# Down product of a decoder step: block results added in pairs by VectorE, other places for plain jobs, buffers shared with the gated layer

## The chip, the cores and the metric

The kernel runs on one core of one Trainium2 chip. The metric is the device time of one execution in microseconds (us), the median of several runs. The engines are TensorE (PE: matmuls; PEld: its weight loads), VectorE (DVE), ScalarE (ACT), GpSimd (POOL) and SyncE (SP), which issues most DMA transfers.

## What is computed

One step of a decoder layer over 512 prompt tokens and 8 x 8 sample tokens, T = 576 columns in all, in float32. Cut to what matters here:

```
u = rms_norm(x, g_mix) @ w_in                 # 2048 -> three mixers' inputs
y_a = short_conv(u_a); y_b = ssd(u_b, dt_bias, a_log, ...); y_c = sparse_attention(u_c)
x = x + concat(rms_norm(y_a), rms_norm(y_b), rms_norm(y_c)) @ w_out
h = rms_norm(x, g_ffn)
x = x + (silu(h @ w_gate) * (h @ w_up)) @ w_down      # 2048 -> 5632 -> 2048
```

## The kernel before

All products run on TensorE with the weights as the stationary operand and 288 of the 576 columns (HALF) as the moving one. A float32 operand is held as two parts, `hi` (made by ScalarE, a copy to fp32r) and `lo` (made by VectorE, operand minus `hi`); one product is hi\*hi + hi\*lo + lo\*hi, so three matmuls for each 128 rows. `split` (line 130) makes the pair.

**Input projection.** `run_jobs` (line 441) runs jobs of 96 matmuls, one for 128 columns of `w_in`, in three lists: `jobs1`, `jobs2`, `jobs3`. Between the matmuls of a job `pump.run(369.0 * len(job.halves) * ratio)` lets `Pump` (line 38) take steps of side work worth that many estimated nanoseconds. The side work is `chain` (line 1664): compress, `sample_attn` (eight batches), `prompt_attn`, `merge_c`. A ratio of 0.85 (`jobs2`) or 1.05 (`jobs3`) sets how much side work goes in for each main matmul, and so how dense the main matmuls lie in the instruction order. Each engine then executes its own list in order.

**Out projection.** `jobs4` multiplies the merged mixers (S4, S3) by `w_out`, with `ssd` (line 1189) and `merge_a` as side work. `ssd` begins with 16 short VectorE operations on `sd`, which need the loads `dtb` (dt_bias) and `ea` (exp of a_log), issued there on SyncE's queue (lines 1194, 1196).

**Gated layer.** `w_gate` and `w_up` are multiplied block-wise by a 2 x 2 scheme of seven products instead of eight. An item is seven products of 12 matmuls, 84 in all; there are 88 items. `prep` makes each product's weight pair; the pairs lie in pool `wpool` (tags whi, wlo, 3 buffers) for three of seven products and in pool `fw` (fhi, flo, 4 buffers) for the others, chosen by a running count (line 1905). Raw weights come in `fw`'s `wr` (5 buffers). The result g goes to DRAM (`g_d`). The pool `fw` is closed at line 1986, before the down product's tiles are opened.

**Down product.** 5632 rows of `w_down` are cut into 16 plain jobs on the first 4 row tiles (`jobs6[0]`, 24 matmuls each), three ranges of twelve tiles, of which eight tiles go through the seven-product scheme (eight items of 84 matmuls, product order "1256473") and four tiles are again 16 plain jobs, and 16 last plain jobs, behind which the output rows are transposed and stored (`out_rows`). In one item:

- `w_ops` makes the seven weight pairs: four VectorE additions of weight blocks (`ws`, `wr`) and seven `lo` subtractions (tile f), from raw tiles `wr` (8 buffers of 128 columns).
- `evac_d` (line 2094) takes each product's sum out of PSUM: x1T (the running result, in SBUF) gets products 2, 3, 4 and 5 by VectorE directly; product 1 goes by ScalarE into u, u becomes 1+6 and then 1+6+7 by VectorE, and GpSimd adds u to x1T three times in an item (two of 288 columns, one of 576).
- PSUM: products 1, 2, 5 in `pt` (3 buffers), 6 and 4 in the two halves of one `pg` tile, 7 in `po`, 3 in a second `pg` tile.

Plain jobs stand behind items of odd number (`mp % 2`, four of eight) in the first two ranges; the other twelve of a range run behind it, mixed with `range_ops` of the next range, which builds that range's 28 combinations of g (tile go). `g_in` loads and splits the four tiles of g for the next plain jobs (tile ghl).

Of the kernel before, what the change touches and what calls it, by code (L numbers as in the profile page):

```python
# [76 lines left out]
def hybrid_step_kernel(ctx, tc, x_prompt, x_sample, cache_k, cache_v, cache_win_k, cache_win_v,  # L77
# [238 lines left out]

    rstdB = consts.tile([128, T], F32, name="rstdB")

    ssq = consts.tile([128, 5], F32, name="ssq")
# [121 lines left out]
    def run_jobs(jobs, ratio):  # L441
        for job in jobs:
            run_group([job], ratio)
# [745 lines left out]
    def ssd():  # L1189
        YB = dp.tile([128, 4, T], F32, name="YB")  # L1190
        sq_b = sq_c
        tiny = lambda name, n=8: dp.tile([128, 5, n], F32, name=name)
        dtb = dp.tile([128, 8], F32, name="dtb")
        nc.sync.dma_start(dtb, dram(dt_bias, 0, [[0, 128], [1, 8]]))
        ea = dp.tile([128, 8], F32, name="ea")
        nc.sync.dma_start(ea, dram(a_log, 0, [[0, 128], [1, 8]]))
        dsk = dp.tile([128, 4], F32, name="dsk")
# [489 lines left out]
    run_jobs(jobs1[2:], 0.8)  # L1687
    run_jobs(jobs2, 0.85)
    run_jobs(jobs3, 1.05)
    pump.drain(main)  # L1690
# [189 lines left out]
    def prep(i):  # L1880
# [16 lines left out]
        for n in "1264375":  # L1897
            if g < NE and n in "12":
                continue
            if n == "6":  # L1900
                s2 = ws(s1, a11, OP.subtract)
            if n == "3":
                s4 = ws(a12, s2, OP.subtract)
            src = {"1": a11, "2": a12, "6": s2, "4": a22, "3": s4, "7": s3, "5": s1}[n]
            p = n_op[0] % 7
            n_op[0] += 1
            pool, pre, bufs = (wpool, "w", 3) if p < 3 else (fw, "f", 4)
            hi = pool.tile([128, KC, 128], F32R, name=pre + "hi", tag=pre + "hi", bufs=bufs)
            lo = pool.tile([128, KC, 128], F32R, name=pre + "lo", tag=pre + "lo", bufs=bufs)
            split(hi, lo, src)  # L1910
            out.append((n, hi, lo))
            tick(600)
            yield
# [71 lines left out]

    close_pool(fwg)
    x1g, x1p = open_pool("x1")
# [14 lines left out]
    def out_rows(m):  # L2002
# [3 lines left out]
        ot = evt(512).rearrange("p (a b) -> p a b", a=4)  # L2006
        ots = fp.tile([128, 128], F32, name="ots", tag="ots", bufs=2)
        ps = pt()
# [54 lines left out]
    def load_d(i):  # L2063
        if i >= len(items):
            return
        r, mp = items[i]
        loaded[i] = []
        for h in range(2):
            for q_ in range(2):
                w = fp.tile([128, KC, 128], F32, name="wr", tag="wr", bufs=8)  # L2070
                nc.sync.dma_start(w, dram(w_down, (12 * r + 4 + 4 * h) * 128 * D + mp * 256 + q_ * 128,
                                          [[D, 128], [128 * D, KC], [1, 128]]))
                loaded[i].append(w)

    def w_ops():

        for i in range(len(items)):
            a11, a21, a12, a22 = loaded.pop(i)
            s1 = fp.tile([128, KC, 128], F32, name="ws", tag="ws", bufs=2)
            for n in ORDER:  # L2080
# [6 lines left out]
                src = {"1": a11, "2": a12, "3": a12, "4": a22, "5": s1, "6": a11, "7": a21}[n]  # L2087
                hi, lo = [fp.tile([128, KC, 128], F32R, name=f"f{q_}", tag=f"f{q_}", bufs=4) for q_ in range(2)]
                split(hi, lo, src)
# [3 lines left out]

    def evac_d(mp, n, p, u):

        m = mp * 2
        x11, x21, x12 = x1T[:, m, :HALF], x1T[:, m + 1, :HALF], x1T[:, m, HALF:]
        if n == "1":
            act(u, p)
            tt(x11, x11, u, OP.add, G)  # L2100
        elif n == "2":
            tt(x11, p, x11, OP.add)
        elif n == "5":
            x2 = x1T[:, m:m + 2, HALF:]
            tt(x2, p[:, None, :].to_broadcast([128, 2, HALF]), x2, OP.add)
        elif n == "6":
            tt(u, p, u, OP.add)
            tt(x12, x12, u, OP.add, G)
        elif n == "4":
            tt(x21, p, x21, OP.add)  # L2110
        elif n == "7":
            tt(u, p, u, OP.add)
            x2 = x1T[:, m + 1].rearrange("p (h t) -> p h t", h=2)
            tt(x2, x2, u[:, None, :].to_broadcast([128, 2, HALF]), OP.add, G)
        else:
            tt(x12, p, x12, OP.add)

# [30 lines left out]
    for r in range(NR):  # L2148
        rest = list(jobs6[1 + r])
        tiles = list(range(plain[1 + r], plain[1 + r] + 4))  # L2150
        for mp in range(KT // 2):
            if r + 1 == NR and mp == 7:
                tiles = list(range(plain[-1], nf))
            i = r * KT // 2 + mp
            u = evt(HALF)
            pa, pb = pg(), pg()
            ps = [pt()[:, :HALF] for _ in range(3)] + [pa[:, 0, :HALF], pa[:, 1, :HALF], po()[:, :HALF], pb[:, 0, :HALF]]
            for p, n in zip(ps, ORDER):
                next(weights, None)
                hi, lo = made.pop((i, n))  # L2160
                for j in range(KC):
                    o = ops[r, j, n]
                    for c_, (w, x) in enumerate(((hi, o[:, 0]), (hi, o[:, 1]), (lo, o[:, 0]))):
                        PE.matmul(p, w[:, j, :], x, start=(j == 0 and c_ == 0), stop=(j == 3 and c_ == 2))  # L2164
                evac_d(mp, n, p, u)
                if tiles and (n in "53" or r + 1 == NR):
                    g_in(tiles.pop(0))

            for _ in range((2, 2, 2, 2, 3, 3, 2, 0)[mp] if r + 1 == NR else mp % 2):
                run_group([rest.pop(0)], 0.0)  # L2170
# [10 lines left out]
    close_pool(fg)  # L2181
    close_pool(x1g)
    close_pool(eg)

# [28 lines left out]
```

## Time and profile before

| | us |
|---|---|
| median of 3 runs (2987.16 to 2991.98) | 2990.16 |
| the profiled execution | 2989.67 |
| its span, first to last instruction | 2987.9 |
| TensorE busy | 2837.6 (95%) |
| VectorE busy | 2170.7 (73%) |
| ScalarE busy | 1283.3 (43%) |
| GpSimd busy | 641.2 (21%) |

By the time line the input projection lasts from 0 to about 1150 us (sample attention 500 to 800, prompt attention to 1130), the out projection from 1150 to 1340, the gated layer from about 1520 to 2426, the down product from 2426 to the end. A window's row gives, for each engine, busy us and in brackets the instructions that began in it. At full clock TensorE does 77 matmuls in 10 us, so a row with fewer tells what was lost, by waiting or by a lower clock.

### The profile page before, as it was taken

To read this page: it belongs to the slowest core of one execution; us is meant where nothing else is said; L and a number is where in the kernel's file an instruction comes from. 1 tells how busy PE (TensorE), PEld (TensorE's weight loads), DVE (VectorE), ACT (ScalarE), POOL (GpSimd) and SP (SyncE) were. 2 spreads that over 40 slices of the span, in tenths; PEclk is the share of its full clock that TensorE was granted. 3 is DMA by queue.
4 is the path that set the end of the run, shared out by engine and by line. 5 is a ranking of instruction groups with operands and counts; after the bars stand their busy time and mean duration, and the time that the engine had idled before them with its cause. 6 is when DMAs were issued, how large, how long until landed. Compare 5 with 4: busy or idle time off the path is not lost.

```text
span 2987.9 us, 57523 instructions
## 1 busy us (share of the span) xinstructions
PE 2837.6 (95%) x22006; PEld 2729.2 (91%) x22006; DVE 2170.7 (73%) x4409; ACT 1283.3 (43%) x2432; POOL 641.2 (21%) x672
## 2 busy tenths in 40 slices
PE   7999998787899998999999999999999999999999
PEld 6999997676789887999999999999999999999998
DVE  5566565444586765757899988888888879889874
ACT  5465563222354553335554444444444434444332
POOL 2342342444343320202001101101101102222120
PEclk9999999898999998999999999999999999999999
DMA  7444333554623214357655433333333354333323
GB/s 234 117 130 124 94 90 84 166 161 144 151 60 79 58 50 138 105 159 215 185 182 172 161 101 108 109 106 108 107 109 109 108 180 125 118 103 118 110 70 111
DMA packets 485660, 370.65 MB, mean 124 GB/s; under 512 B 70121, under 2 KB 444880, under 8 KB 485384
## 3 DMA queue, kind: packets, MB, share of 16 engines
q1 hardware_dynamic: 461656, 306.55, 35.2%
q0 software_dynamic: 20944, 55.13, 6.4%
q10 hardware_dynamic: 2784, 5.29, 0.5%
q8 instruction: 174, 2.85, 0.4%
q14 instruction: 102, 0.84, 0.1%
HBM read 312.98 MB, written 51.79 MB: 122 GB/s over the span
## 4 chain that ended last, share of the span: by engine, by line
PE 49%; DVE 5%; DMA 2%; issue 1%; ACT 1%; SPq 0%; POOL 0%; ACTq 0%; DVEq 0%
PE pg L1949 16%; PE pg L434 12%; PE pt L1949 9%; PE po L1949 5%; PE pg L2164 2%; PE pt L2164 2%; DVE f L96 1%; PE pt L434 1%; PE po L2164 1%; DVE wlo L96 1%; DVE x1T L96 1%; DMA raw<-in_w_up_dram 1%; DMA u<-g_d 1%; DVE wr L96 0%; PE pt L128 0%
## 5 line engine op out<-in xcount | busy, mean ns | idle before, releaser
L93 ACT ACTIVATE whi<-raw 128x512 fp32r<-128x512 f32 (+1 forms) x510 | 319.4, 628 | 536.8 <-PE pg L434 260.7
L96 DVE TENSOR_TENSOR wlo<-raw,whi 128x512 fp32r<-128x512 f32 (+1 forms) x510 | 354.1, 696 | 171.3 <-ACT whi L93 143.3
L434 PE MATMUL pg<-hhi,whi 128*128 128x288 f32 (+1 forms) x1440 | 344.6, 319 | 4.8 <-issue 4.0
L1949 PE MATMUL pg<-X,fhi 128*128 128x288 f32 x1656 | 333.6, 297 | 0.5 <-DVE u L96 0.5
L434 PE MATMUL pg<-hlo,whi 128*128 128x288 f32 (+1 forms) x1440 | 326.0, 306 | 8.1 <-issue 4.7
L434 PE MATMUL pg<-hhi,wlo 128*128 128x288 f32 (+1 forms) x1440 | 324.1, 305 | 7.3 <-issue 4.3
L1949 PEld LDWEIGHTS pg<-X,fhi 128*128 128x128 f32 x1656 | 264.8, 188 | 4.5 <-DVE u L96 0.7
L96 POOL TENSOR_TENSOR u<-u 128x576 f32<-128x576 f32 x44 | 70.9, 1616 | 888.3 <-DVE u L96 811.2
L434 PEld LDWEIGHTS pg<-hhi,whi 128*128 128x128 f32 (+1 forms) x1440 | 238.0, 196 | 20.7 <-issue 17.0
L434 PEld LDWEIGHTS pg<-hlo,whi 128*128 128x128 f32 (+1 forms) x1440 | 241.8, 196 | 13.5 <-issue 8.7
L434 PEld LDWEIGHTS pg<-hhi,wlo 128*128 128x128 f32 (+1 forms) x1440 | 241.5, 196 | 9.6 <-issue 5.9
L93 ACT ACTIVATE fhi<-raw 128x512 fp32r<-128x512 f32 x246 | 155.3, 632 | 212.1 <-PE pg L1949 180.9
L1949 PE MATMUL pg<-X,flo 128*128 128x288 f32 x828 | 239.3, 295 | 0.0
L1949 PE MATMUL pt<-X,whi 128*128 128x288 f32 x1168 | 235.8, 295 | 0.0
L434 PE MATMUL pg<-ghl,whi 128*128 128x288 f32 x1280 | 228.8, 298 | 3.9 <-DVE ghl L96 2.6
L96 DVE TENSOR_TENSOR flo<-raw,fhi 128x512 fp32r<-128x512 f32 x246 | 170.2, 693 | 46.3 <-ACT fhi L93 41.9
L434 PE MATMUL pg<-S,whi 128*128 128x288 f32 x1024 | 197.1, 301 | 0.4 <-DVE u L96 0.4
L434 PEld LDWEIGHTS pg<-ghl,whi 128*128 128x128 f32 x1280 | 190.1, 190 | 4.9 <-DVE ghl L96 2.8
L1949 PEld LDWEIGHTS pt<-X,whi 128*128 128x128 f32 x1168 | 188.2, 188 | 0.0
L96 POOL TENSOR_TENSOR x1T<-x1T,u 128x288 f32<-128x288 f32 (+1 forms) x72 | 99.1, 1376 | 392.7 <-ACT u L93 240.5
L1949 PE MATMUL pt<-X,wlo 128*128 128x288 f32 x584 | 172.9, 296 | 0.0
L434 PEld LDWEIGHTS pg<-S,whi 128*128 128x128 f32 x1024 | 159.0, 191 | 1.4 <-issue 0.6
(1343 smaller groups left out, 6979.0 us busy)
## 6 DMA issues: line engine op xcount, KB each, us to landing
wr<-in_w_gate_dram SPq DMA_DIRECT2D x88, 512.0 KB
wr<-in_w_up_dram SPq DMA_DIRECT2D x88, 512.0 KB
raw<-in_w_in_dram SPq DMA_DIRECT2D x144, 256.0 KB
wr<-in_w_down_dram SPq DMA_DIRECT2D x96, 256.0 KB
raw<-in_w_down_dram SPq DMA_DIRECT2D x80, 256.0 KB
raw<-in_w_out_dram SPq DMA_DIRECT2D x64, 256.0 KB
g_d<-u POOLq DMA_DIRECT2D x44, 288.0 KB
u<-g_d SPq DMA_DIRECT2D x40, 288.0 KB
```

What stands on the lines that cost most here:

```text
L93: S.activation(out, in_, func, bias=bias, scale=scale, accum_out=accum)
L96: (eng or V).tensor_tensor(out, a, b, op=op)
L434: PE.matmul(ps[:m, s, :HALF], w[:, k, :m], x[:, s * HALF:(s + 1) * HALF], start=(k0 + k == 0 and n == 0), stop=(k0 + k == n_k - 1 and n == 2))
L1949: PE.matmul(P[n], w[:, k, :], xx, start=(j == 0 and q_ == 0), stop=(j == 7 and q_ == 2))
L2164: PE.matmul(p, w[:, j, :], x, start=(j == 0 and c_ == 0), stop=(j == 3 and c_ == 2))
```

## The change

1. `ea` and `dtb` become constants of the program, loaded on GpSimd's queue near its start, and not inside `ssd` on SyncE's queue.
2. The ratios of `jobs2` and `jobs3` go from 0.85 to 0.95 and from 1.05 to 1.1: more side work for each main matmul, so the chain ends earlier in the order and more main matmuls are left behind it.
3. The gated layer's last item takes its first three products from `wpool` and its last four from `fw`.
4. `fw` stays open. The down product's raw weights lie in its `wr` (5 buffers of 256 columns), and its weight pairs in its fhi, flo (4 buffers).
5. `ots`, the staging tile of the sample rows, has one buffer and not two.
6. `evac_d` uses no GpSimd. Products 2 and 3 share one `pg` tile and are added to x1T by one VectorE addition of 576 columns; product 1 and 1+6 lie side by side in u and are added in one addition of 576; 1+6+7 is made in a tile v and added in one of 576. Product 4 is in `po`, 1, 5, 6 and 7 are in `pt`.
7. Plain jobs stand behind six of eight items (`mp % 4 > 0`) in the first two ranges, and in the last range as (0, 2, 3, 4, 4, 3, 0, 0) and not (2, 2, 2, 2, 3, 3, 2, 0). Ten jobs, not twelve, then carry `range_ops`, three steps each. The tiles of g for the last jobs are asked for from item 6 on, and always behind products 5 and 3.

```diff
+    nc.gpsimd.dma_start(ea, dram(a_log, 0, [[0, 128], [1, 8]]))
+    nc.gpsimd.dma_start(dtb, dram(dt_bias, 0, [[0, 128], [1, 8]]))
...
-        nc.sync.dma_start(dtb, dram(dt_bias, 0, [[0, 128], [1, 8]]))
-        nc.sync.dma_start(ea, dram(a_log, 0, [[0, 128], [1, 8]]))
...
-    run_jobs(jobs2, 0.85)
-    run_jobs(jobs3, 1.05)
+    run_jobs(jobs2, 0.95)
+    run_jobs(jobs3, 1.1)
...
-            p = n_op[0] % 7
+            p = n_op[0] % 7 if i + 1 < len(items) else len(out)
...
-    close_pool(fwg)
...
-        ots = fp.tile([128, 128], F32, name="ots", tag="ots", bufs=2)
+        ots = fp.tile([128, 128], F32, name="ots", tag="ots", bufs=1)
...
+            w2 = fw.tile([128, KC, 256], F32, name="wr", tag="wr", bufs=5).rearrange("p a b -> p (a b)")
...
-                w = fp.tile([128, KC, 128], F32, name="wr", tag="wr", bufs=8)
+                w = w2[:, q_ * KC * 128:(q_ + 1) * KC * 128].rearrange("p (k c) -> p k c", k=KC)
...
-                hi, lo = [fp.tile([128, KC, 128], F32R, name=f"f{q_}", tag=f"f{q_}", bufs=4) for q_ in range(2)]
+                hi, lo = [fw.tile([128, KC, 128], F32R, name=q_, tag=q_, bufs=4) for q_ in ("fhi", "flo")]
...
         if n == "1":
-            act(u, p)
-            tt(x11, x11, u, OP.add, G)
-        elif n == "2":
-            tt(x11, p, x11, OP.add)
+            act(u[:, :HALF], p)
...
-            tt(u, p, u, OP.add)
-            tt(x12, x12, u, OP.add, G)
+            tt(u[:, HALF:], p, u[:, :HALF], OP.add)
...
-            tt(u, p, u, OP.add)
+            v = evt(HALF)
+            tt(v, p, u[:, HALF:], OP.add)
             x2 = x1T[:, m + 1].rearrange("p (h t) -> p h t", h=2)
-            tt(x2, x2, u[:, None, :].to_broadcast([128, 2, HALF]), OP.add, G)
-        else:
-            tt(x12, p, x12, OP.add)
+            tt(x2, x2, v[:, None, :].to_broadcast([128, 2, HALF]), OP.add)
+            tt(x1T[:, m], x1T[:, m], u, OP.add)
+        elif n == "3":
+            tt(x1_, p23, x1_, OP.add)
...
-            pa, pb = pg(), pg()
-            ps = [pt()[:, :HALF] for _ in range(3)] + [pa[:, 0, :HALF], pa[:, 1, :HALF], po()[:, :HALF], pb[:, 0, :HALF]]
+            pa = pg()
+            p1, p5, p6 = [pt()[:, :HALF] for _ in range(3)]
+            ps = [p1, pa[:, 0, :HALF], p5, p6, po()[:, :HALF], None, pa[:, 1, :HALF]]
...
-            for _ in range((2, 2, 2, 2, 3, 3, 2, 0)[mp] if r + 1 == NR else mp % 2):
+            for _ in range((0, 2, 3, 4, 4, 3, 0, 0)[mp] if r + 1 == NR else mp % 4 > 0):
```

Two places show how the order moves. The first is TensorE in one down item, from the end of product 6 to the start of product 3. Before (f_29520 and f_29521 are product 6's pair, f_29559 and f_29560 product 7's, f_29537 and f_29538 product 4's):

```order
L2164 MATMUL pg<-go,f_29521 128x288
L2164 MATMUL po<-go,f_29559 128x288 [waits Activation_49]
...
L2164 MATMUL po<-go,f_29559 128x288 x2
L2164 MATMUL pg<-go,f_29537 128x288 [waits DVE_49]
...
L2164 MATMUL pg<-go,f_29538 128x288
L2164 MATMUL po<-go,f_29560 128x288
...
L2164 MATMUL pg<-go,f_29577 128x288 [waits Activation_49]
```

Now, products 4 (po), 7 (pt) and 3 (pg) of an item:

```order
L2165 MATMUL po<-go,fhi 128x288 [waits Activation_49]
L2165 MATMUL po<-go,fhi 128x288
L2165 MATMUL po<-go,flo 128x288 [waits DVE_49]
...
L2165 MATMUL pt<-go,fhi 128x288 [waits Activation_49]
L2165 MATMUL pt<-go,fhi 128x288
L2165 MATMUL pt<-go,flo 128x288 [waits DVE_49]
...
L2165 MATMUL pg<-go,fhi 128x288 [waits Activation_49]
L2165 MATMUL pg<-go,fhi 128x288
L2165 MATMUL pg<-go,flo 128x288 [waits DVE_49]
```

Before, product 4's first matmul waits for VectorE, which must first have taken product 6 out of the same tile, and product 7's twelve matmuls are cut in two around it; now each product waits for nothing but its own weights.

The second is VectorE where the out projection begins: the last evacuations of the input projection (x<-pg) and the head of `ssd`'s operations on sd. Before:

```order
L96 TENSOR_TENSOR wlo<-raw,whi 128x512 [waits DMAHW6_49,DMAHW7_49,PE_49,Activation_49]
L96 TENSOR_TENSOR x_13438<-pg,x_13438 128x288 [waits DMAHW0_49,PE_49]
L96 TENSOR_TENSOR x_13446<-pg,x_13446 128x288 [waits DMAHW2_49,DMAHW1_49]
L96 TENSOR_TENSOR x_13439<-pg,x_13439 128x288 [waits DMAHW3_49,PE_49]
L96 TENSOR_TENSOR sd_13534<-dtg,dtb 128x40 [waits DMAHW3_49]
L96 TENSOR_TENSOR x_13447<-pg,x_13447 128x288 [waits DMAHW5_49,DMAHW4_49]
L105 SCALAR_TENSOR_TENSOR sd_13535<-sd_13534 128x40 [waits DVE_49]
```

Now:

```order
L96 TENSOR_TENSOR wlo<-raw,whi 128x512 [waits DMAHW6_49,Activation_49]
L96 TENSOR_TENSOR u<-u,rstdB 128x576 [waits DVE_49]
L1412 COPY u<-cols_198 128x8x2
L96 TENSOR_TENSOR sd_13534<-dtg,dtb 128x40
L100 TENSOR_SCALAR triU<-diff 128x128
L105 SCALAR_TENSOR_TENSOR sd_13535<-sd_13534 128x40 [waits DVE_49]
L100 TENSOR_SCALAR sd_13539<-sd_13534 128x40
```

The sd operations no longer wait for a load, and they stand ahead of the input projection's last evacuation and not behind the out projection's first results (the x<-pg). On TensorE, 201 main matmuls of the input projection now stand behind the last matmul of `merge_c`, where 54 stood; and in each of the eight batches of the sample attention 96 main matmuls stand where 108 stood.

## Rows read from the trace of the kernel before

**Rows 1.** Windows by stage: sample attention, then prompt attention and its end.
```profile
500.00:780.00 280.00, 216.55 (x2044) 178.61 (x2040) 116.13 (x327) 61.93 (x114) 123.81 (x130) 0.85 0.51 153
860.00:1150.00 290.00, 285.12 (x2384) 257.92 (x2383) 204.69 (x649) 143.79 (x361) 88.93 (x89) 1.00 0.26 61
```

**Rows 2.** Windows (PE, PEld, DVE, ACT, POOL; PEclk): start of the out projection.
```profile
1150.00:1195.00 45.00, 32.40 (x179) 30.04 (x178) 25.47 (x80) 9.22 (x20) 5.22 (x6) 0.73 0.69 200
...
1165.00:1170.00 5.00, 5.00 (x40) 5.00 (x39) 0.82 (x2) 0.21 (x1) 0.00 (x0) 1.00 0.66 193
```

**Rows 3.** Waits in 1145 to 1200: engine, line, what ended it: us, times, longest.
```profile
ACT ea L93 <- DMA ea<-in_a_log_dram: 6.9, 1, 6.9
...
PE pt L120 <- DVE sd L105: 6.6, 1, 6.6
...
PE pg L434 <- DVE wlo L96: 4.9, 1, 4.9
```

**Rows 4.** Time line of VectorE there: start, duration, operation.
```profile
1172.35 0.19 DVE L96 TENSOR_TENSOR sd<-dtg,dtb 128x40 f32<-128x40 f32 x1
...
1178.30 0.20 DVE L105 SCALAR_TENSOR_TENSOR sd<-sd,ea 128x40 f32<-128x40 f32 x1
```

**Rows 5.** Time line of SyncE's queue there: the next weights of the out projection.
```profile
1176.51 1.92 SPq L1721 DMA_DIRECT2D raw<-in_w_out_dram  x3
```

**Rows 6.** Waits of TensorE, 500 to 820.
```profile
PE po L120 <- issue: 14.8, 27, 1.8
```

**Rows 7.** Windows over the down product.
```profile
2426.00:2590.00 164.00, 155.68 (x1121) 153.04 (x1120) 143.26 (x235) 67.58 (x125) 35.07 (x27) 0.97 0.52 158
2590.00:2750.00 160.00, 156.81 (x1165) 154.97 (x1165) 144.56 (x241) 66.04 (x125) 35.33 (x25) 1.00 0.37 109
2750.00:2910.00 160.00, 160.00 (x1197) 159.11 (x1196) 127.10 (x204) 58.32 (x105) 29.24 (x21) 1.00 0.32 94
```

**Rows 8.** Windows of 10 us at four places of it.
```profile
2420.00:2430.00 10.00, 6.96 (x50) 6.37 (x48) 5.21 (x8) 2.92 (x5) 3.20 (x3) 0.97 0.73 234
2430.00:2440.00 10.00, 9.31 (x51) 9.31 (x52) 4.70 (x8) 1.60 (x4) 1.08 (x3) 0.69 0.87 287
...
2580.00:2590.00 10.00, 8.23 (x51) 8.00 (x50) 7.70 (x15) 3.54 (x7) 1.36 (x2) 0.83 0.69 223
...
2910.00:2920.00 10.00, 8.78 (x66) 8.55 (x65) 6.77 (x11) 4.93 (x8) 2.01 (x2) 1.00 0.45 146
...
2940.00:2950.00 10.00, 10.00 (x79) 9.89 (x78) 4.95 (x9) 3.43 (x6) 0.00 (x0) 1.00 0.46 133
```

**Rows 9.** Waits in 2400 to 2988.
```profile
PE pg L2164 <- DVE u L96: 8.4, 9, 1.8
...
ACT go L93 <- DMA u<-g_d: 6.9, 4, 2.2
```

**Rows 10.** Time line of ScalarE and of VectorE where the down product begins.
```profile
2426.07 0.63 ACT L93 ACTIVATE whi<-raw 128x512 fp32r<-128x512 f32 x1 [7.48 <-PE po L1949]
...
2428.69 3.95 DVE L96 TENSOR_TENSOR ghl<-go,ghl 128x576 fp32r<-128x576 f32 x4
```

**Rows 11.** VectorE's groups by form, 2490 to 2580 (seven items).
```profile
L96 DVE TENSOR_TENSOR f<-wr,f 128x512 fp32r<-128x512 f32 x40 | 28.3, 710 | 0.3
L96 DVE TENSOR_TENSOR f<-ws,f 128x512 fp32r<-128x512 f32 x7 | 13.5, 1923 | 0.0
...
L96 DVE TENSOR_TENSOR wr<-ws,wr 128x512 f32<-128x512 f32 x7 | 7.3, 1039 | 0.2
...
L96 DVE TENSOR_TENSOR x1T<-pt,x1T 128x576 f32<-128x576 f32 x7 | 5.2, 750 | 0.4 <-PE pt L2164 0.2
```

**Rows 12.** Time line of VectorE in an item, 2510.
```profile
2510.14 1.92 DVE L96 TENSOR_TENSOR f<-ws,f 128x512 fp32r<-128x512 f32 x1
2511.98 0.44 DVE L96 TENSOR_TENSOR x1T<-pg,x1T 128x288 f32<-128x288 f32 x1
```

**Rows 13.** Time line of GpSimd there.
```profile
2509.70 1.81 POOL L96 TENSOR_TENSOR x1T<-x1T,u 128x576 f32<-128x576 f32 x1 [3.07 <-DVE u L96]
```

More of the change, by code (lines that the diff above doesn't have):

```diff
@@ L317, in hybrid_step_kernel @@
     rstdB = consts.tile([128, T], F32, name="rstdB")
+    ea = consts.tile([128, 8], F32, name="ea")
+    dtb = consts.tile([128, 8], F32, name="dtb")
+    nc.gpsimd.dma_start(ea, dram(a_log, 0, [[0, 128], [1, 8]]))
+    nc.gpsimd.dma_start(dtb, dram(dt_bias, 0, [[0, 128], [1, 8]]))
     ssq = consts.tile([128, 5], F32, name="ssq")
@@ L1192, in ssd @@
         tiny = lambda name, n=8: dp.tile([128, 5, n], F32, name=name)
-        dtb = dp.tile([128, 8], F32, name="dtb")
-        nc.sync.dma_start(dtb, dram(dt_bias, 0, [[0, 128], [1, 8]]))
-        ea = dp.tile([128, 8], F32, name="ea")
-        nc.sync.dma_start(ea, dram(a_log, 0, [[0, 128], [1, 8]]))
         dsk = dp.tile([128, 4], F32, name="dsk")
@@ L2092, in w_ops, with evac_d @@
             load_d(i + 2)
-    def evac_d(mp, n, p, u):
+    def evac_d(mp, n, p, u, p23):
         m = mp * 2
-        x11, x21, x12 = x1T[:, m, :HALF], x1T[:, m + 1, :HALF], x1T[:, m, HALF:]
+        x21, x1_ = x1T[:, m + 1, :HALF], x1T[:, m].rearrange("p (h t) -> p h t", h=2)
         if n == "1":
-            act(u, p)
-            tt(x11, x11, u, OP.add, G)
-        elif n == "2":
-            tt(x11, p, x11, OP.add)
+            act(u[:, :HALF], p)
         elif n == "5":
@@ L2151, in hybrid_step_kernel @@
         for mp in range(KT // 2):
-            if r + 1 == NR and mp == 7:
+            if r + 1 == NR and mp == 6:
                 tiles = list(range(plain[-1], nf))
             i = r * KT // 2 + mp
-            u = evt(HALF)
-            pa, pb = pg(), pg()
-            ps = [pt()[:, :HALF] for _ in range(3)] + [pa[:, 0, :HALF], pa[:, 1, :HALF], po()[:, :HALF], pb[:, 0, :HALF]]
+            u = evt(T)
+            pa = pg()
+            p1, p5, p6 = [pt()[:, :HALF] for _ in range(3)]
+            ps = [p1, pa[:, 0, :HALF], p5, p6, po()[:, :HALF], None, pa[:, 1, :HALF]]
             for p, n in zip(ps, ORDER):
+                p = pt()[:, :HALF] if p is None else p
                 next(weights, None)
@@ L2164, in hybrid_step_kernel @@
                         PE.matmul(p, w[:, j, :], x, start=(j == 0 and c_ == 0), stop=(j == 3 and c_ == 2))
-                evac_d(mp, n, p, u)
-                if tiles and (n in "53" or r + 1 == NR):
+                evac_d(mp, n, p, u, pa[:, :, :HALF])
+                if tiles and n in "53":
                     g_in(tiles.pop(0))
-            for _ in range((2, 2, 2, 2, 3, 3, 2, 0)[mp] if r + 1 == NR else mp % 2):
+            for _ in range((0, 2, 3, 4, 4, 3, 0, 0)[mp] if r + 1 == NR else mp % 4 > 0):
                 run_group([rest.pop(0)], 0.0)
@@ L2182, in hybrid_step_kernel @@
     close_pool(x1g)
+    close_pool(fwg)
     close_pool(eg)
```

## The prediction

> **What bounds the kernel now.** I read the stages first. In the gated layer, which the change leaves alone but for its last item, TensorE has no gap; the time can only move where it has. The windows over the down product [rows 7] give the yardstick: the last 160 us hold 1197 matmuls, 7.48 in a microsecond or 0.134 us each, and that is full speed. By it the first 164 us could hold 1227 and hold 1121, so 106 are missing, 14.2 us; the next 160 us miss 32, 4.3 us. Of the rest one window, 2910, is short, with 66 for the 77 of a full one [rows 8]: 11 matmuls, 1.5 us. So 20.0 us are lost in the down product. Three places take most of it. Its start (windows 2420 and 2430) has 50 and 51 for 77 and 77: 53 matmuls, 7.1 us, with a granted clock of 0.69 behind the pause [rows 8]. The step into the second range, 2580, has 51, 3.5 us. The window at 2910 is 1.5. What is left, 20.0 - 7.1 - 3.5 - 1.5 = 7.9 us, lies inside the items, and the waits name it: nine times TensorE waits for VectorE's u, 8.4 us in all [rows 9].
>
> The second place is the start of the out projection. The 45 us from 1150 hold 179 matmuls [rows 2]; at 7.48 they could hold 337, so 158 are missing, 21 us. The waits [rows 3] give two of the reasons: 4.9 us for a wlo of VectorE, which is behind with `merge_c`, and 6.6 us for sd. The rest, some 9.5 us, is clock: 0.73 over the stretch, after TensorE had stood still.
>
> **The start of the out projection (parts 1 and 2).** Now the sd operations run from 1172.35 to 1178.30 [rows 4], with TensorE waiting; their load ea makes ScalarE wait 6.9 us [rows 3]. With the loads far ahead and the higher ratios, sd stands on VectorE ahead of the input projection's end, and 201 main matmuls cover `merge_c` and the beginning of `ssd` where 54 did. That is 147 x 0.134 = 19.7 us of cover for a hole of 21. I take that both waits go, 11.5 us, and a quarter of the clock's 9.5, together **-14**. Bounds: all the cover works, -19.7; or only the sd wait goes, -6.6. What is late next are the weights: SyncE issues the out projection's next raw chunks only at 1176.51 [rows 5], behind the x loads, and one chunk more now stands ahead of them; a wait of 0 to 3 us is left there, which the -14 allows for.
>
> This is not free, because main matmuls are only moved. In the sample attention, TensorE is busy 216.55 of 280 us at a clock of 0.85 [rows 1]: the side chain paces it, and main matmuls fill what is open. Each of the eight batches has 12 fewer, 8 x 12 x 0.134 = 12.9 us of TensorE work that goes to the end. If the chain alone sets the time of a batch, the stage keeps its length and all 12.9 are paid; if each step of the chain queues on TensorE behind the main matmuls ahead of it, the stage gets shorter by as much and nothing is paid. TensorE's waits there are of both kinds, with 14.8 us in 27 short ones for nothing that shows [rows 6]. I take **+5**, nearer to the lower half, since in 216.55 of 280 us TensorE is what is being used; bounds 0 and 12.9. In the prompt attention TensorE is busy 285.12 of 290 at full clock [rows 1]; slightly denser side work there must be hidden by main matmuls that are still there: **+1**, 0 to 4 (the idle of that row is 4.9 and may at worst nearly double).
>
> The loads themselves: two small ones at the beginning of GpSimd's queue stand ahead of the first gathers, and `ea` is wanted a thousand us later; 0.
>
> **Inside the down items (parts 6 and 7).** What the change takes away on TensorE's side is plain: product 4 had to wait until VectorE had taken product 6 out of the same PSUM tile; now 4 has its own and 2 and 3 share one that nobody reads until both are done. What it does on VectorE's side needs prices. From a start to the next, VectorE's instructions lie 0.08 closer than they last (2510.14 + 1.92 = 2512.06, and the next begins at 2511.98 [rows 12]). Undisturbed, 512 columns last 0.68 and so cost 0.60; the 576-column PSUM addition lasts 0.75 [rows 11] and costs 0.67; a 288-column one 0.45, so 0.37. Before, an item has 11 operations on weights, 6.6 us, and takes results out in 5 x 0.37 + 0.67 = 2.5: 9.1. On top come the disturbed ones: f<-ws lasts 1.92 and not 0.68, wr<-ws,wr 1.04, and f<-wr a mean of 0.71 [rows 11]; 1.24 + 0.36 + 7 x 0.03, some 1.8 in all, so 10.9 of the 11.2 (84 x 0.134) that TensorE needs. The long f<-ws begins while GpSimd is in its 576-column addition, from 2509.70 for 1.81 to 2511.51 [rows 13], and ends 0.55 after it. After, results cost 5: 0.67, 6: 0.37, 7: 0.37 + 0.67 + 0.67, 4: 0.37, 3: 0.67, in all 3.8; the two additions wholly in SBUF have no row of this size, and I price them as the 512-column ones by width. That is 6.6 + 3.8 = 10.4 with no GpSimd beside it: about the same work, but no piece of 1.9 us before which an evacuation stands still. A plain job brings VectorE 1.27 us (a wlo and an addition of 576) for 3.2 of TensorE, so six jobs in eight items, not four, leave more slack: 10.4 + 0.75 x 1.27 = 11.4 for 13.6. Of the 7.9 us I take **-7**; bounds -4 (half the waits come back as waits for weights) and -7.9.
>
> The added wait: the addition for product 3 now holds back product 2 as well, and behind it on VectorE stand the next item's first lo parts, which are made ahead; nobody waits.
>
> Beside this stands a rule. The Trainium skill, page "SBUF — State Buffer", section "Who interferes with whom", says that VectorE with two SBUF inputs and GpSimd reading SBUF share one pair of ports, and that who has it holds it for the whole instruction. By that rule the long f<-ws is GpSimd's doing and goes with it, and the sum stays; the trace agrees so far as 2511.51 lies inside the long one. If the length were f<-ws's own, see the third rival.
>
> **The start of the down product (parts 3 and 4).** ScalarE makes the fourth whi only at 2426.07, when the gated layer's last product in `po` has ended, after 7.48 us of waiting; the g tiles' splits are queued behind it, and VectorE's four ghl run from 2428.69 for 3.95 [rows 10]. TensorE stands still, and the clock falls. With the last item's first three products in `wpool`, the whi buffers come free three products into it, and the last products in `fw` hold no one up; the splits of g then wait for their loads alone. What is late next are the g tiles' four ghl on VectorE behind the layer's last evacuations: 1 to 2 us. I take **-5.5** of 7.1; bounds -2 and -7.1. That the down weights share `fw`'s buffers costs nothing here: their first item comes 16 plain jobs, 51 us, later.
>
> **The rest.** At 2580 the go operations wait for loads of g_d (6.9 us in four waits [rows 9]) which stand in SyncE's queue behind raw weights that wait for buffers; with five wide buffers and no wait for GpSimd these loads come sooner: **-2**, 0 to -3.5. At 2910 the last g tiles come an item earlier: **-1**, 0 to -1.5. `ots` with one buffer makes VectorE's copy wait for the store of the job before, with the next evacuation behind it; VectorE is busy 4.95 of 10 us at 2940 [rows 8], which covers it: 0, and 1 at most.
>
> **Sum**, against the profiled execution's own 2989.67 (span 2987.9, with 1.8 around it; the median is 0.5 above): -14 + 5 + 1 - 7 - 5.5 - 2 - 1 = -23.5, so **2966**. All terms at their good bounds: -19.7 - 7.9 - 7.1 - 3.5 - 1.5 = -39.7, 2950; at their bad ones -6.6 + 12.9 + 4 - 4 - 2 + 1 = +5, 2995.
>
> **Rivals.** *The main matmuls are only moved.* The batches of the sample attention are paced by their own chain, 12.9 is paid, prompt attention pays 2, and the out projection begins with a wait for weights and gets 8: -8 + 12.9 + 2 - 15.5 = -8.6, 2981. For it: TensorE idles a fifth of that stage. Against: 11.5 us of the hole are waits that the new order takes out by name. 0.2.
>
> *VectorE's long pieces are its own.* Then f<-ws keeps 1.84 and wr<-ws,wr 0.96, and an item costs 10.4 + 1.6 = 12.0, over TensorE's 11.2; with the plain jobs 12.95 for 13.6, so the items still pass, with waits. Of -7 some -3 is left: 2970. Against: the coincidence in [rows 12, 13]. 0.1.
>
> *The clock, slower than before.* The sample attention runs at 0.85 [rows 1]. With fewer main matmuls between its steps TensorE pauses longer, and the clock falls further. The gains make -29.5; it decides from 216.55 x (0.85 / c - 1) = 29.5, so c = 0.75. At 0.70 it costs 46.4: 2989.7 - 29.5 + 46.4 = 3007. Against: a ninth fewer main matmuls is little. 0.06.
>
> *The buffers don't free the start.* If a g tile's load or the splits are still late, the 7.1 us stay: 2971.5. 0.08.
>
> **How the numbers follow.** The forecast has 0.56. The good bounds give 2950 and the first rival 2981; leaving out the slow case and the ends of both, the range is 2952 to 2984. About 6 us, 0.2%, is what a measurement here can tell from no change. Slower by that: the clock case beyond its point, 0.05. Within it: the first rival with two terms at their bad bounds, 0.07. Faster: 0.88.
>
> **What would show it.** In the profile after: the 45 us behind `merge_c` have 280 matmuls or more and no wait for sd; the sample attention lasts at most 5 us longer and its clock stays at 0.82 or above; f<-ws (now flo<-ws) lasts 0.7 and TensorE doesn't wait for u; the two windows at the down product's start miss under 20 matmuls; GpSimd does nothing in the down items. A down product no shorter by 10 us, or a sample attention longer by over 13, would make the prediction wrong.

## The result and the profile after

| | us |
|---|---|
| before, median of 4 runs (2987.16 to 2991.98) | 2989.69 |
| changed, median of 4 runs (2951.75 to 2959.47) | 2958.52 |
| ratio, 95% interval | 0.9891, 0.9874 to 0.9908 |
| changed: profiled execution, and its span | 2951.75, 2949.9 |

The change takes 31 us off, 1.1%. The prediction was 2966, with a range of 2952 to 2984: right in sign and range, with a gain of 31 where 23.5 was forecast. Of the four executions of `late_loads` below, one took 4446.98 us at a granted clock of 0.557 and is left out of its figures.

The profiled execution is the shortest of the four; the stages below are its own. Where the time went is read from marks that both traces have, the first or last matmul on a named tile: the stage's time is then the same measure in every kernel below.

| stage (us) | before | changed | difference |
|---|---|---|---|
| sample attention: first KC_s to last ob | 309.0 | 298.0 | -11.0 |
| prompt attention: last ob to last kh | 302.1 | 297.0 | -5.1 |
| rest of the input projection: last kh to last hhi | 41.4 | 64.3 | +22.9 |
| out projection and early gate: last hhi to first X | 280.2 | 260.2 | -20.0 |
| gated layer: first X to last X | 992.7 | 994.3 | +1.6 |
| down product: last X to last ghl | 558.5 | 536.9 | -21.6 |

These make 33.2 of the 37.9 us between the two profiled executions; 4.4 of the others lie ahead of the sample attention, whose first matmul comes anywhere from 491.8 to 500.7 in the kernels that did not run on chip 0, whatever their edit. How far a stage repeats: the down product takes 536.5 to 537.2 us in the four kernels that have it as changed, and 557.6 to 561.3 in the four that have it as before.

The windows of the changed kernel over the start of the out projection, which answers to [rows 2], and over the down product, which answer to [rows 7] (columns as there: window, its length, PE, PEld, DVE, ACT, POOL, then PEclk, which is TensorE's granted clock as a share of full speed, the DMA share and GB/s):

```profile
1150.00:1195.00 45.00, 43.35 (x335) 41.39 (x334) 30.60 (x77) 15.60 (x28) 8.17 (x6) 1.00 0.99 239
```

```profile
2406.00:2570.00 164.00, 163.42 (x1223) 162.49 (x1222) 144.41 (x251) 69.39 (x127) 4.43 (x4) 1.00 0.50 155
2570.00:2730.00 160.00, 160.00 (x1206) 160.00 (x1205) 145.35 (x264) 70.00 (x133) 0.00 (x0) 1.00 0.39 118
2730.00:2890.00 160.00, 160.00 (x1207) 159.98 (x1206) 123.01 (x207) 59.18 (x103) 0.00 (x0) 1.00 0.30 89
```

The 45 us hold 335 matmuls where 179 were, at full clock and not at 0.73. The down product's windows hold 1223, 1206 and 1207 where 1121, 1165 and 1197 were. Its TensorE has two waits left in the list of waits from 2400 on:

```profile
PE pt L128 <- issue: 0.9, 1, 0.9
PE pg L438 <- DVE u L96: 0.4, 1, 0.4
```

and VectorE's groups by form, 2474 to 2564, which answer to [rows 11]:

```profile
L96 DVE TENSOR_TENSOR flo<-wr,fhi 128x512 fp32r<-128x512 f32 x41 | 28.0, 687 | 6.8 <-ACT fhi L93 6.3
L96 DVE TENSOR_TENSOR x1T<-x1T,u 128x576 f32<-128x576 f32 x13 | 9.8, 750 | 0.0
...
L96 DVE TENSOR_TENSOR flo<-ws,fhi 128x512 fp32r<-128x512 f32 x7 | 4.8, 681 | 0.0
L96 DVE TENSOR_TENSOR wr<-ws,wr 128x512 f32<-128x512 f32 x6 | 4.1, 683 | 0.0
```

The long f<-ws of 1923 ns is now 681, wr<-ws,wr fell from 1039 to 683, and the two additions wholly in SBUF, which no row of before priced, last 750: at 0.08 less from start to start that is the 0.67 that the prediction took. VectorE even has 6.8 us of idle time ahead of its lo parts in 90 us. Where the down product begins, which answers to [rows 10], ScalarE:

```profile
2408.46 0.63 ACT L93 ACTIVATE fhi<-ws 128x512 fp32r<-128x512 f32 x1 [0.96 <-PE pg L1950]
2409.00 0.69 ACT L93 ACTIVATE ghl<-go 128x576 fp32r<-128x576 f32 x1
2410.79 2.09 ACT L93 ACTIVATE ghl<-go 128x576 fp32r<-128x576 f32 x3 [1.11 <-DMA go<-g_d]
```

Nothing stands in the way of the first ghl any more; the three others wait for a load, 1.11 us. TensorE goes from the gated layer's last product to the first plain job with a wait of 0.4.

### The profile page after: what moved, and what is told of

It reads as the page before. It is cut to its first block, busy times and chain, and to the rows that moved or that the text cites. A ratio compares the mean times of both kernels' runs of the same rounds, so it can differ in the third digit from the quotient of the medians.

```text
span 2949.9 us, 57376 instructions
## 1 busy us (share of the span) xinstructions
PE 2821.5 (96%) x22006; PEld 2716.9 (92%) x22006; DVE 2162.2 (73%) x4433; ACT 1284.5 (44%) x2432; POOL 545.4 (18%) x602
## 4 chain that ended last, share of the span: by engine, by line
PE 53%; DVE 2%; DMA 1%; ACT 1%; issue 0%; SPq 0%; POOL 0%; ACTq 0%; DVEq 0%
PE pg L1950 17%; PE pg L438 12%; PE pt L1950 9%; PE pt L2165 5%; PE po L1950 5%; PE pg L2165 3%; PE po L2165 1%; DVE wlo L96 1%; DMA raw<-in_w_out_dram 1%; PE pt L438 1%; DMA raw<-in_w_up_dram 1%; PE pt L128 0%; DMA raw<-in_w_gate_dram 0%; PE pt L120 0%; ACT whi L93 0%
## 5 line engine op out<-in xcount | busy, mean ns | idle before, releaser
L93 ACT ACTIVATE fhi<-wr 128x512 fp32r<-128x512 f32 x222 | 140.4, 632 | 221.8 <-PE pg L1950 89.0
L96 DVE TENSOR_TENSOR flo<-wr,fhi 128x512 fp32r<-128x512 f32 x222 | 155.7, 703 | 63.2 <-ACT fhi L93 61.5
```

Source lines behind the costliest of these rows:

```text
L93: S.activation(out, in_, func, bias=bias, scale=scale, accum_out=accum)
L96: (eng or V).tensor_tensor(out, a, b, op=op)
```

## Experiments

All ratios are to the kernel before, run beside each group of kernels on the same chip: chip 6 for the first four, chip 11 for the next four, chip 0 for the last four (for the result above it is not known). So each table gives before's median of its own. "Down product" is the stage of the table above.

**The two places apart.** Which of the 31 us belong to the down product's side (parts 3 to 7), and which to the front (parts 1 and 2)?

> Parts 3 to 7 alone (the whole down product's side), on the kernel before. If the two places are independent, the down product takes 537 us as in the changed kernel and not 558.5, and all before 2420 us stays: 2990 - 21 = 2969, between 2966 and 2973. Rival, the parts help each other (a shorter front lets the loads come sooner): less than 15 us.

`start_only` has the front alone:

> Parts 1 and 2 alone (ratios and the two loads), on the kernel before. If independent: the rest of the changed kernel's gain, 31 - 21 = 10 us by the medians, up to 17 by the two profiled executions, so 2973 to 2980. Sample attention shorter by about 11 us, the out projection by 20, the input projection's last main matmul 2 us later.

```diff
-    run_jobs(jobs2, 0.85)
-    run_jobs(jobs3, 1.05)
+    run_jobs(jobs2, 0.95)
+    run_jobs(jobs3, 1.1)
```

`ratios_only` has only these four lines, `loads_only` only the moved loads of ea and dtb:

> Part 2 alone: ratios 0.95 and 1.1, loads of dtb and ea still in ssd. If the main matmuls that now stand behind merge_c fill the hole, most of the gain of parts 1 and 2 is here: 2975 to 2982, with a wait of ScalarE for ea that TensorE doesn't feel. If the load was what mattered, TensorE still waits some 6 us for sd and the gain is under 6 us: above 2984.

> Part 1 alone: dtb and ea loaded early, ratios as before. If the hole is a matter of order, sd still stands behind the last evacuations on VectorE and its 6 us run with TensorE waiting: a gain of 0 to 3 us, 2987 to 2990. If the load is the cause, the sd wait of 6.6 us and the half clock behind it go: 2978 to 2982.

| kernel | median | ratio, interval | sample att. | prompt att. | rest of input proj. | out proj. | down product |
|---|---|---|---|---|---|---|---|
| before | 2987.7 | | 309.0 | 302.1 | 41.4 | 280.2 | 558.5 |
| down_only | 2962.73 | 0.9927, 0.9910 to 0.9945 | 305.4 | 302.1 | 41.4 | 278.4 | 536.6 |
| start_only | 2981.14 | 0.9983, 0.9971 to 0.9995 | 300.9 | 297.2 | 64.2 | 260.8 | 560.7 |
| ratios_only | 2978.77 | 0.9971, 0.9957 to 0.9985 | 295.8 | 297.1 | 64.2 | 261.7 | 561.3 |
| loads_only | 2988.96 | 1.0014, 1.0001 to 1.0027 | 308.9 | 302.2 | 41.3 | 277.5 | 557.6 |

(The stages are those of the profiled executions; before's are those of its one profile.) The two places are independent as far as the stages repeat: the new down product takes 536.6 with the front of before and 536.9 with the new one, the old one 558.5 and 561. By the ratios the down side brings 0.7%, some 22 us, and the front 0.2 to 0.3%, 5 to 9 us. `down_only` came out below its range though its stage was as expected, and `start_only` 1 us above its own.

The front is the ratios' work. Their windows for 1150 to 1195, `ratios_only`, then `loads_only`:

```profile
1150.00:1195.00 45.00, 41.94 (x320) 39.25 (x319) 30.47 (x83) 14.84 (x27) 7.52 (x6) 1.00 0.84 239
```

```profile
1150.00:1195.00 45.00, 32.08 (x204) 29.36 (x203) 28.63 (x85) 11.21 (x22) 5.52 (x6) 0.85 0.74 217
```

With the ratios alone the hole is nearly full, 320 of the changed kernel's 335; with the loads alone it has 204 for 179. The loads do take ScalarE's wait for ea away (none is in the list), and TensorE's wait for sd falls from 6.6 to 1.7 us, in the waits of `loads_only`:

```profile
PE pg L438 <- DVE wlo L96: 4.9, 1, 4.9
...
PE pg L438 <- ACT whi L93: 2.8, 1, 2.8
...
PE pt L120 <- DVE sd L105: 1.7, 1, 1.7
```

but the wait for wlo, behind `merge_c`, stays at 4.9 and a new one of 2.8 stands beside it. The stage is 2.7 us shorter, of which the run's time shows nothing: by its interval it is 0.0 to 0.3% slower than before. So the load was not the cause of the hole; the order was.

**What the results' way out of PSUM is worth.** Three kernels take part 6 apart. `old_evac` is the changed kernel with the old `evac_d` and the old PSUM tiles; `ve_old_tiles` is the same with the three additions on VectorE:

```diff
-            tt(x11, x11, u, OP.add, G)
+            tt(x11, x11, u, OP.add)
...
-            tt(x12, x12, u, OP.add, G)
+            tt(x12, x12, u, OP.add)
...
-            tt(x2, x2, u[:, None, :].to_broadcast([128, 2, HALF]), OP.add, G)
+            tt(x2, x2, u[:, None, :].to_broadcast([128, 2, HALF]), OP.add)
```

`gp_scratch` is the changed kernel with three more additions on GpSimd, whose result nobody uses:

```diff
             act(u[:, :HALF], p)
+            tt(rstdB[:, :HALF], rstdB[:, :HALF], u[:, :HALF], OP.add, G)
...
             tt(u[:, HALF:], p, u[:, :HALF], OP.add)
+            tt(rstdB[:, HALF:], rstdB[:, HALF:], u[:, HALF:], OP.add, G)
...
+            r2 = rstdB.rearrange("p (h t) -> p h t", h=2)
+            tt(r2, r2, v[:, None, :].to_broadcast([128, 2, HALF]), OP.add, G)
```

> The changed kernel with part 6 undone: results taken out as before, three GpSimd additions an item, product 4 in product 6's tile; all else as changed. Theory (GpSimd's additions stretch VectorE, and the shared tile hands that on to TensorE): f<-ws is 1.9 us again, TensorE waits for u again, and with more plain jobs beside the items 4 to 8 us come back: 2963 to 2967 by the median of 2958.5. Rival (the plain jobs' places and the start were what counted): under 2 us.

> As old_evac, but the three additions on VectorE and not on GpSimd; product 4 still waits for product 6 to be taken out of its tile. VectorE's work in an item is then 9.1 + 0.37 + 0.37 + 0.67 = 10.5 us by the prices of before. Theory: no long f<-ws, 0.7 us each, and the wait for u stays short, so within 2 us of the changed kernel: 2958 to 2961. Rival (the shared tile by itself is the cause): as slow as old_evac.

> The changed kernel, with GpSimd besides making three additions an item, of the same sizes as before and reading u and v, into a tile that nobody uses. If two engines reading SBUF get in each other's way, flo<-ws and others are stretched to 1.2 to 1.9 us, some 1.8 us an item, and VectorE needs 12.2 us for an item of 11.2: with the plain jobs just under TensorE's pace, 3 to 10 us slower, 2962 to 2969. Rival (the long f<-ws had another cause): all stay at 0.68 and the time is the changed kernel's, 2958.5.

| kernel (before: 2985.73) | median | ratio, interval | down product |
|---|---|---|---|
| old_evac | 2974.25 | 0.9955, 0.9940 to 0.9970 | 553.1 |
| ve_old_tiles | 2964.53 | 0.9929, 0.9912 to 0.9946 | 541.0 |
| gp_scratch | 2979.97 | 0.9977, 0.9968 to 0.9987 | 556.8 |
| changed (before: 2989.69) | 2958.52 | 0.9891, 0.9874 to 0.9908 | 536.9 |

So of the 16.2 us that come back in the down product with the old way out, 12.1 are GpSimd's (553.1 against 541.0), and 4.1 the tiles' and the unpaired additions'. By the medians, with `old_places` (2958.02, below) for the changed kernel on this chip, the split is 9.7 and 6.5, so it is known to some 2 us. Both were expected smaller: 4 to 8 us for the whole, and at most 2 for `ve_old_tiles`. GpSimd's part has two ways of working in it, for VectorE also waits for GpSimd's results, in the waits of `old_evac`:

```profile
DVE x1T L96 <- POOL x1T L96: 12.0, 17, 0.7
```

These waits are gone in `ve_old_tiles`; what each way costs TensorE can't be read from these two kernels. The shared tile with its wait for u does little harm while VectorE is quick. In `ve_old_tiles` TensorE waits for u 0.5 us in all, in `old_evac` 6.7; the same line of the list of waits, `old_evac` first:

```profile
PE pg L2165 <- DVE u L96: 6.7, 7, 1.8
```

```profile
PE pg L2165 <- DVE u L96: 0.5, 2, 0.4
```

`gp_scratch` shows the cause by itself. No engine waits there for GpSimd's additions, nor for the buffers that they read, and none of the changed kernel's operations is altered; yet the kernel takes 22 us more than `old_places`, which is as fast as the changed kernel. VectorE's groups there, 2477 to 2567, and GpSimd's:

```profile
L96 DVE TENSOR_TENSOR x1T<-x1T,u 128x576 f32<-128x576 f32 x13 | 21.7, 1668 | 0.0
...
L96 DVE TENSOR_TENSOR flo<-ws,fhi 128x512 fp32r<-128x512 f32 x7 | 4.7, 676 | 0.0
```

```profile
L96 POOL TENSOR_TENSOR rstdB<-rstdB,u 128x288 f32<-128x288 f32 x12 | 13.9, 1155 | 47.4 <-DVE u L96 26.2 <-ACT u L93 21.2
L96 POOL TENSOR_TENSOR rstdB<-rstdB,u 128x576 f32<-128x576 f32 x7 | 12.2, 1740 | 17.9 <-DVE u L96 17.9
```

Now it is x1T<-x1T,u that lasts 1668 and not 750, and flo<-ws keeps its 676. In `old_evac`, 2482 to 2572, it is others, with means of short and long ones:

```profile
L96 DVE TENSOR_TENSOR wr<-wr 128x512 f32<-128x512 f32 x14 | 16.8, 1202 | 0.0
...
L96 DVE TENSOR_TENSOR flo<-ws,fhi 128x512 fp32r<-128x512 f32 x7 | 7.2, 1031 | 0.0
```

So the length belongs to no operation. In the down product of `gp_scratch`, 65 VectorE additions with two SBUF inputs begin while GpSimd is in one of its own; all of them last until 0.5 to 0.6 us after its end. One case, VectorE and GpSimd in `gp_scratch`:

```profile
2489.33 0.68 DVE L96 TENSOR_TENSOR wr<-wr 128x512 f32<-128x512 f32 x1
2489.93 1.97 DVE L96 TENSOR_TENSOR x1T<-x1T,u 128x576 f32<-128x576 f32 x1
```

```profile
2489.56 1.72 POOL L96 TENSOR_TENSOR rstdB<-rstdB,u 128x576 f32<-128x576 f32 x1 [1.73 <-DVE u L96]
```

GpSimd is done at 2491.28; the addition, begun at 2489.93, ends at 2491.90, 0.62 later, about the 0.67 that it needs by itself. The Trainium skill (page "SBUF — State Buffer", section "Who interferes with whom") says that VectorE with two SBUF inputs and GpSimd reading SBUF exclude each other, and that who issues first has the shared ports for the whole instruction. The trace agrees, and in the other direction too. In `old_evac` three of GpSimd's additions of 288 columns take 2.47 us and not the 0.8 to 1.4 of the rest; each begins 0.16 us behind an addition of VectorE, and VectorE's next ones keep their length. GpSimd and VectorE at one of them:

```profile
2492.51 2.47 POOL L96 TENSOR_TENSOR x1T<-x1T,u 128x288 f32<-128x288 f32 x1 [5.70 <-DVE u L96]
```

```profile
2492.35 0.68 DVE L96 TENSOR_TENSOR flo<-wr,fhi 128x512 fp32r<-128x512 f32 x1
2492.95 0.75 DVE L96 TENSOR_TENSOR ghl<-u,ghl 128x576 fp32r<-128x576 f32 x1
2493.62 0.68 DVE L96 TENSOR_TENSOR wr<-ws,wr 128x512 f32<-128x512 f32 x1
```

The groups that read PSUM keep their length: in `gp_scratch` x1T<-pg of 576 columns has a mean of 747 ns. The effect was expected; its price for TensorE was not. I had put 3 to 10 us on it and it is 20 in the stage. Windows over the items of the first and of the second range:

```profile
2459.00:2559.00 100.00, 97.65 (x709) 96.69 (x708) 91.68 (x131) 38.04 (x64) 25.30 (x19) 0.97 0.32 96
...
2619.00:2719.00 100.00, 97.07 (x715) 96.27 (x714) 98.20 (x140) 38.08 (x64) 27.59 (x21) 0.98 0.32 94
```

Both hold 40 to 47 matmuls fewer than the 756 and 755 of the changed kernel, at a granted clock of 0.97 and 0.98. In the second VectorE was busy 98.20 of 100 us, so the pieces of 1.2 to 2 us had no slack to go into; in the first it had 8 us of slack and TensorE lost as much. TensorE's longest waits in this down product are for the plain jobs:

```profile
PE pg L438 <- ACT ghl L93: 3.7, 3, 2.0
PE pg L438 <- DVE ghl L96: 3.4, 3, 1.9
PE pg L438 <- DVE x1T L96: 2.8, 4, 0.9
```

That is 9.9 of the 20 us; the rest is lower clock and gaps that the list doesn't name, and wasn't taken apart.

**The plain jobs' places.**

> The changed kernel with plain jobs behind four of eight items, not six, in the first two ranges (the last range as changed). VectorE needs 10.4 us for an item of 11.2, so it keeps up without the extra jobs: no difference, within 1.5 us of 2958.5. Rival (VectorE lives on the slack of the plain jobs): TensorE waits again inside the items, 3 to 6 us slower.

```diff
-            for _ in range((0, 2, 3, 4, 4, 3, 0, 0)[mp] if r + 1 == NR else mp % 4 > 0):
+            for _ in range((0, 2, 3, 4, 4, 3, 0, 0)[mp] if r + 1 == NR else mp % 2):
```

2958.02, ratio 0.9905 (0.9889 to 0.9922), down product 537.3: no difference, as expected. Here, where VectorE needs less than TensorE for an item, more plain jobs beside it buy nothing. The window over items of the first range holds 756 matmuls in 100 us with four jobs, as it does with six (the last range's new places were not undone by themselves):

```profile
2464.00:2564.00 100.00, 100.00 (x756) 100.00 (x756) 88.28 (x146) 40.91 (x69) 0.00 (x0) 1.00 0.36 106
```

**The start, the items together, and the front once more.** These four ran on chip 0, on which the kernel before takes 2875.7; the ratio and the stages are to be compared, not the times.

> The changed kernel with part 3 undone: the gated layer's last item takes its pairs by the running count, so that its last products may lie in wpool. If the start of the down product was blocked by these buffers, ScalarE waits some 7 us for po again before the g tiles' splits, and 4 to 5.5 us come back: 2962 to 2964. Rival (the shared fw or the order alone freed the start): within 1.5 us of 2958.5.

```diff
-            p = n_op[0] % 7 if i + 1 < len(items) else len(out)
+            p = n_op[0] % 7
```

> The changed kernel with parts 6 and 7 undone: results and plain jobs as before, down weights in fw. The difference to the changed kernel is what the items alone brought, that to the kernel before with the ratios (2979 to 2981) what the shared buffers brought. old_evac gave +16 us with the new places; with the old ones, which gave VectorE more room in the last range, +8 to +13: 2967 to 2972. Rival (the new places matter with GpSimd as much as without): as old_evac, 2974.

(The edit is `old_evac`'s, with the plain jobs' places and the tiles' loads as in the kernel before.)

> The changed kernel with part 1 undone, dtb and ea loaded in ssd by SyncE. By ratios_only against start_only, no loss and perhaps a gain of 1 to 3 us: 2955 to 2959. Rival (the early loads count once sd stands early): a wait of TensorE for sd, 2 to 5 us slower.

> The changed kernel with ratios 1.05 and 1.15, so still more main matmuls behind merge_c. The hole at 1150 to 1195 is full, so more cover buys nothing there, while sample attention loses cover: its stage gets shorter by less than the matmuls moved. 0 to 6 us slower, 2958 to 2965. Rival (the chain's steps queue behind main matmuls, so that fewer of them cost nothing): 2953 to 2958.

| kernel (before: 2875.7) | median | ratio, interval | sample att. | out proj. | down product |
|---|---|---|---|---|---|
| old_last_item | 2845.22 | 0.9889, 0.9873 to 0.9906 | 198.3 | 261.5 | 540.8 |
| old_items | 2855.74 | 0.9935, 0.9918 to 0.9951 | 193.9 | 261.0 | 551.1 |
| late_loads (three executions) | 2838.44 | 0.9876, 0.9856 to 0.9895 | 195.9 | 261.7 | 536.5 |
| high_ratios | 2840.45 | 0.9879, 0.9862 to 0.9895 | 185.1 | 257.9 | 537.2 |

`old_items` brings 14.2 of the down product's 21.6 us back (551.1 against 536.9), a little over the 8 to 13 expected. `old_last_item` is 3.9 us longer there and by the medians 5 to 7 us behind `high_ratios` and `late_loads`, with intervals that overlap. But it doesn't lose them where part 3 should count. The first 20 us of the down product and the next 20, of `old_last_item` and of `late_loads`:

```profile
2304.00:2324.00 20.00, 19.28 (x141) 18.56 (x140) 18.37 (x31) 8.07 (x15) 4.43 (x4) 1.00 0.84 277
2324.00:2344.00 20.00, 17.76 (x122) 17.55 (x121) 16.42 (x36) 9.00 (x21) 0.00 (x0) 0.91 0.91 279
```

```profile
2293.00:2313.00 20.00, 19.36 (x141) 18.69 (x141) 18.90 (x32) 8.90 (x16) 4.43 (x4) 1.00 0.92 294
2313.00:2333.00 20.00, 19.94 (x150) 19.74 (x149) 18.34 (x40) 9.93 (x24) 0.00 (x0) 1.00 0.86 280
```

At the start both have 141 matmuls, where the kernel before has 102. What is lost comes later, 122 against 150, and the waits of `old_last_item` in 2326 to 2352 give one late load of a plain job's weights:

```profile
ACT whi L93 <- DMA raw<-in_w_down_dram: 3.4, 1, 3.4
...
PE pg L438 <- DVE x1T L96: 2.2, 1, 2.2
```

So the start is free without part 3, and whether that late load comes from the edit or from this one execution can't be told from one profile. It is free without the new items too (139 in the first 20 us of `old_items`) and without the new front (141 in `down_only`). By exclusion it is the shared `fw` (part 4) that frees the start; it was not undone by itself. It may work through the buffers or only through the order, for in `old_last_item` ScalarE has a ghl ahead of the whi which in the kernel before came first and held all four up:

```profile
2306.79 0.67 ACT L93 ACTIVATE ghl<-go 128x576 fp32r<-128x576 f32 x1
2308.37 0.63 ACT L93 ACTIVATE whi<-raw 128x512 fp32r<-128x512 f32 x1 [0.91 <-ACT ghl L93]
```

`late_loads` tells the same of the loads as before: moving them brings nothing that these runs can show. `high_ratios` is as fast as `late_loads`: with 346 main matmuls behind `merge_c` and not 201 sample attention is 10.8 us shorter and the out projection 3.8, and the time does not change, where I had expected 0 to 6 us more. On chip 0 the ratio is on a plateau; on the others this was not run.

## Why the prediction was right, and where its sum was off

**The out projection's start, -14.** The stage became 20.0 us shorter in the two profiles and 18 as a mean over the kernels with new and old ratios that did not run on chip 0 (seven against three). The waits named for it, sd and wlo, went with the order: in `ratios_only` TensorE waits 1.1 us for wlo and not at all for sd. The term was a little small, since nearly all of the clock's 9.5 us went as well, where I had counted a quarter: the granted clock over the 45 us is 1.00 for 0.73.

**The price, +5 and +1.** The moved matmuls, put at 19.7 us, make the rest of the input projection 22.9 longer, and the two attention stages became shorter by 9.4 (the same mean) and 5.0. So 8.5 were paid and 6 forecast. Of the 12.9 us taken out of the sample attention three quarters came back and 3.5 were paid, less than the 5 forecast, which fits a side chain whose steps queue on TensorE behind the main matmuls ahead of them. Some 6.8 us (the other 51 of the 147 matmuls) were taken out of the prompt attention and 1.8 paid there. The remaining 3.2 are a term that the forecast did not have: the stage to which the matmuls were moved runs at a lower clock. It is, before and changed:

```profile
1108.40:1149.80 41.40, 40.95 (x356) 38.80 (x356) 23.52 (x48) 20.34 (x38) 1.31 (x2) 1.00 0.17 46
```

```profile
1087.90:1152.20 64.30, 63.04 (x503) 60.74 (x502) 43.29 (x102) 26.32 (x47) 3.05 (x6) 0.95 0.28 71
```

The granted clock is 0.95 and not 1.00, and 5% of 64.3 us is 3.2. The front as a whole was forecast at -8; the means give -18 + 22.9 - 9.4 - 5 = -9.5. That this came out near is in part luck, since the gain and the price were both taken too small.

**The items, -7.** This is the step that failed. `old_items` puts it at 14.2 us and `old_evac` at 16.2. The mechanism was the one named: GpSimd's additions stretch VectorE's instructions with two SBUF inputs, and through u and the shared tile TensorE waits. The mis-sizing is, for a good part, in the yardstick: "the last 160 us hold 1197 matmuls ... and that is full speed". It was not. The changed kernel does 1206 and 1207 in 160 us, so by that yardstick the windows of [rows 7] miss 116, 41 and 9 matmuls, not 106, 32 and 0: 22.0 us with 7.54 a microsecond, and 23.5 with the window at 2910. With the three places taken off (7.0, 3.4 and 1.5) 11.6 us are left for the items, and not 7.9; the 14.2 to 16.2 measured are still 3 to 5 more. The 0.8% that a "full" stretch hid is in gaps too short for the list of waits; no matmul is missing from either trace, with 2016 of the items and 1920 of the plain jobs in each. `ve_old_tiles` has such gaps without GpSimd; its groups of matmuls on pg, in 2463 to 2563, and those of the changed kernel in 2456 to 2556:

```profile
L2165 PE MATMUL pg<-go,fhi 128*128 128x288 f32 x168 | 34.7, 299 | 0.0
```

```profile
L2165 PE MATMUL pg<-go,fhi 128*128 128x288 f32 x112 | 22.6, 295 | 0.0
```

4 ns more in each of 168 is 0.7 us in 100, most of the 8 matmuls by which that window has 748 for 756. That these lie at product 4's start, cut into product 7, fits the order but was not tried by itself. Not explained, and part of the 3 to 5 us, is that `old_items` and `old_evac` miss some 22 matmuls in the last range's items (884 and 883 for 905 in 120 us), where the kernel before, with the same additions, has 898 at the same place.

**The start, -5.5.** The first 20 us hold 142 matmuls for 102 (windows from 2406 and from 2422), 5.3 us at 7.54. The size is right; of the two parts it was put on, part 3 is not needed for it, and part 4 is left by exclusion.

**The rest, -2 and -1.** The pauses at the step into the second range and at 2910 are gone: no window after misses what those did. With 5.3 for the start and 14.2 for the items 2.1 us are left of 21.6 for both, less than the 3.4 and 1.5 that they had cost; the measures come from different kernels and need not add up. `ots` with one buffer makes VectorE wait once for a store, 1.1 us, and nothing of it shows in the time.

**The rivals.** Main matmuls only moved: 8.5 were paid, but the hole gave 18. VectorE's long pieces its own: excluded by `gp_scratch`, where flo<-ws is short and another is long. The clock of the sample attention: 0.85 before [rows 1], 0.84 in the same window after and 0.85 over the whole stage, far from the 0.75 at which this rival would have taken the gain.

```profile
493.00:791.00 298.00, 234.25 (x2276) 192.21 (x2276) 127.15 (x360) 69.48 (x128) 131.85 (x139) 0.85 0.49 151
```

Of the change's seven parts three carry the gain: the ratios, the way out of PSUM without GpSimd, and the shared `fw`. The loads and the plain jobs' places in the first two ranges bring nothing that the runs show, and for the last item's pairs it stays open. The staging buffer and the last range's places were not tried by themselves.

## What to carry to other kernels

An engine that helps is not free when it reads the same memory: price a GpSimd addition by what it does to VectorE's instructions with two SBUF inputs, and try it on VectorE when VectorE has time left. Here VectorE took over GpSimd's additions and was still busy only 86 to 90% of the time over the items of the first two ranges. A hole at the end of a stage is filled by keeping main work back for it, and part of the price can come back where the side chain had queued behind that work, as 14 of 23 us did here. Take the full rate for a count of lost matmuls from a stretch where the weight loads have no gap either, not from the best one in sight.

## What the runs showed of the hardware that was not expected

The kernel before takes 2986 to 2990 us on chips 6 and 11 and in the first runs, and 2875.7 on chip 0. The profiled kernels show the stage in which they differ, the sample attention, 298 us against 196 with the same work; the window of `late_loads` on chip 0 beside the one of the changed kernel above:

```profile
483.00:679.00 196.00, 193.00 (x2275) 166.85 (x2275) 125.71 (x363) 70.06 (x128) 135.45 (x139) 0.99 0.75 229
```

The engines' busy times are alike but for TensorE's, and 2275 matmuls stand against 2276; the DMA moves 229 GB/s and not 151, and TensorE is busy 98% of the stage at a granted clock of 0.99, not 79% at 0.85. In the changed kernel's trace three of the stage's five largest sums of waits are put down to no instruction of this core ("remote"); two of them:

```profile
DVE ss L96 <- remote: 44.1, 5, 9.2
...
ACT whi L93 <- remote: 32.8, 4, 18.5
```

On chip 0 there are none of that kind among the largest. What holds the others up is not shown here. The changed down product takes the same on both, 536.9 us and 536.5 and 537.2.
